# The second FFN's up projection from seven products of quarters, with weight sums made by adding transfers in DRAM

## The chip, the cores and the metric

The kernel runs on one core of one Trainium2 chip. The metric is the device time of one execution in microseconds; several runs are made, and their median counts. The engines are TensorE (PE, with its weight loads, PEld), VectorE (DVE), ScalarE (ACT), GpSimd (POOL), and SyncE (SP), which issues the loads.

## What is computed

A block of two layers over 512 latent tokens and 256 context tokens, 1024 channels wide, all in float32. Layer 0 mixes by gated convolutions, layer 1 by windowed attention; each is followed by an FFN with a short convolution:

```python
def conv_ffn(h, w_up, conv, w_down):
    u = dwconv(h @ w_up, conv)              # w_up: 1024 x 5632, three taps along the tokens
    a, g = jnp.split(u, 2, axis=-1)
    return (jax.nn.silu(g) * a) @ w_down    # w_down: 2816 x 1024

x = x + g1 * y                              # y: the mixer of the layer
x = x + g2 * conv_ffn(modulate(rmsnorm(x, norm_ffn[l]), sh2, sc2), w_up[l], w_conv_ffn[l], w_down[l])
```

The modulation (shift, scale, gate) is a matrix product of the conditioning with `w_mod`. The second layer's FFN sees the 512 latent tokens alone.

## The kernel before

Activations lie with channels on the partitions: eight tiles of 128 channels by the tokens. Every float32 operand of a large product is split into two `float32r` tiles: `split` lets ACT make the high part (L159) and DVE the low part (L160). `mm3` (L175) then makes one product of a 128 x 128 weight block by three matmuls: low weight by high input, high by low, high by high (L177 to L179).

A weight tile of 128 rows by 1024 is loaded by SP into one of three buffers `wraw` (L165, in `weights`) and split; the loads run one tile ahead of the products.

`run` goes through the stages: `start` (x, the first modulation pieces through `mod_piece`, the norm, the first projections), `layer0_input` and `layer0_output` (the convolution mixer: the taps on DVE at L578, pads of `ub` zeroed by POOL at L568, a sum `cs` made by POOL at L584 that `conv_norm` reads at L622), the first FFN (`ffn(0)`, 776 columns: 512 and 256), attention, and the second FFN (`ffn(1)`, 512 columns). POOL's small work in `inverse` (L296 to L301) stands in front of each norm.

In `ffn` the 22 pairs f of up-projection tiles (part 0 is `a`, part 1 is `g`) run in five groups (`GROUPS`: 4, 4, 4, 5 and 5 pairs). For the second FFN the first three pairs are made by `side_by_side` in halves of 256 columns, as the halves of h become ready; each other pair takes two `wide_gemm`s of 8 x 3 = 24 matmuls of 512 columns. `conv3` (L368 on ACT, L370 twice on DVE) is done for each part, then silu (L704), a product (L705) and a split give g. After the first pair of the next group, the eight output tiles of the group before are projected down (`down`: split, matmuls, `gate_in` at L360). The last group goes through `project`. `mod_rows` makes modulation columns that are wanted later out of rows of `w_mod` on DVE (L254, `wmod` loads at L250), a row at a time from a list `todo` that `do` works off.

The order of each engine's instructions is fixed when the kernel is built. A scheduler goes through the program by its own estimate of the times; an engine that is free takes the earliest instruction of the program that has its operands and its buffer. `tc.issue_after(ins)` adds an order to that: by its definition in the framework, what its block traces on the engine of `ins` is queued behind `ins`, and instructions of other engines in the block are left as they are. `self.mark` is the last split's instruction on DVE (L160).

## Time and profile before

| | us |
|---|---|
| median of 3 runs | 1472.71 (1472.37 to 1472.92) |
| the profiled execution, its own time | 1473.53 |
| its span, first to last instruction | 1471.8 |
| TensorE busy in the span | 1435.4 |
| DVE busy in the span | 1024.4 |
| mean granted TensorE clock | 0.997 of full |

The page shows one profiled execution. A busy PE is not a PE at its peak, since matmuls overlap: the distance from the start of one to the start of the next tells what one costs. What a stage is bound by is read from the stage's own stretch and not from the share of the whole span.

### The profile page before, as it was taken

How to read it: one execution, taken by the hardware profiler on the slowest of the kernel's cores; microseconds unless marked ns; L12 is line 12 of the kernel's file. 1: busy time of each engine (PE TensorE's matmuls, PEld its weight loads, DVE VectorE, ACT ScalarE, POOL GpSimd, SP SyncE). 2: the span in 40 equal slices, each digit the busy share in tenths (PEclk: the TensorE clock that was granted, in tenths of full speed). 3: DMA queues.
4: the chain of work that ended last, by engine and by line, in shares of the span. 5: the costliest groups of instructions: out<-in, count | busy, mean ns of one | idle time of the engine just before them, and what ended most of it. 6: DMA issues, size and time to landing. Idle time of an engine off the chain costs nothing.

```text
span 1471.8 us, 21937 instructions
## 1 busy us (share of the span) xinstructions
PE 1435.4 (98%) x8786; PEld 1228.8 (83%) x8786; DVE 1024.4 (70%) x1635; ACT 596.9 (41%) x983; POOL 47.8 (3%) x186
## 2 busy tenths in 40 slices
PE   5999999999999999999999999999999999999997
PEld 3888888888888888888888878768799888888887
DVE  6699998689977756456434689786676865655456
ACT  5421224463223223133123475786764442424245
POOL 0000001110000000000000110010001000000000
PEclk9999999999999999999999999999999999999999
DMA  9325433134544532333211324011155333233222
GB/s 374 111 70 173 158 115 130 31 113 146 168 132 127 186 106 81 120 125 91 81 47 43 106 91 125 14 40 58 42 174 163 90 112 98 84 114 97 94 80 74
DMA packets 52709, 161.25 MB, mean 110 GB/s; under 512 B 6400, under 2 KB 6528, under 8 KB 52480
## 3 DMA queue, kind: packets, MB, share of 16 engines
q1 hardware_dynamic: 52608, 159.87, 33.4%
q8 instruction: 68, 1.11, 0.3%
q14 instruction: 33, 0.27, 0.1%
HBM read 155.13 MB, written 2.10 MB: 107 GB/s over the span
## 4 chain that ended last, share of the span: by engine, by line
PE 91%; DVE 4%; ACT 2%; issue 1%; DMA 1%; POOL 1%; DVEq 0%; SPq 0%; ACTq 0%; POOLq 0%
PE slot L177 21%; PE slot L178 21%; PE slot L179 21%; PE av L178 3%; PE av L177 3%; PE av L179 3%; PE av L929 2%; PE pt L919 2%; PE s L900 2%; PE pt L179 2%; PE pt L178 2%; PE pt L177 2%; PE slot L226 1%; PE slot L212 1%; PE slot L208 1%
## 5 line engine op out<-in xcount | busy, mean ns | idle before, releaser
L177 PE MATMUL slot<-h,wlo 128*128 128x512 f32 (+1 forms) x1192 | 410.5, 346 | 2.2 <-DVE ub L570 1.2
L178 PE MATMUL slot<-h,whi 128*128 128x512 f32 (+1 forms) x1192 | 410.8, 345 | 0.2 <-DVE h L350 0.2
L179 PE MATMUL slot<-h,whi 128*128 128x512 f32 (+1 forms) x1192 | 410.8, 345 | 0.0
L159 ACT CAST whi<-wraw 128x1024 fp32r<-128x1024 f32 (+2 forms) x215 | 192.2, 902 | 208.5 <-PE slot L179 109.3
L177 PEld LDWEIGHTS slot<-h,wlo 128*128 128x128 f32 x1192 | 223.5, 188 | 34.3 <-issue 2.0
L178 PEld LDWEIGHTS slot<-h,whi 128*128 128x128 f32 x1192 | 224.1, 188 | 29.0 <-DVE h L350 0.5
L179 PEld LDWEIGHTS slot<-h,whi 128*128 128x128 f32 x1192 | 224.1, 188 | 27.6
L160 DVE TENSOR_TENSOR wlo<-wraw,whi 128x1024 fp32r<-128x1024 f32 (+2 forms) x215 | 222.2, 1040 | 25.1 <-ACT whi L159 24.6
L370 DVE SCALAR_TENSOR_TENSOR cf<-slot,par,cf 128x775 f32<-128x775 f32 (+1 forms) x132 | 122.7, 932 | 136.5 <-ACT cf L368 136.0
L177 PE MATMUL slot<-gh,wlo 128*128 128x512 f32 (+1 forms) x459 | 156.7, 342 | 0.7 <-DVE x L360 0.4
L178 PE MATMUL slot<-gl,whi 128*128 128x512 f32 (+1 forms) x459 | 155.5, 339 | 0.0
L179 PE MATMUL slot<-gh,whi 128*128 128x512 f32 (+1 forms) x459 | 155.1, 339 | 0.0
L368 ACT ACTIVATE cf<-slot,par 128x776 f32<-128x776 f32 (+1 forms) x66 | 55.3, 837 | 243.1 <-PE slot L179 230.7
L360 DVE SCALAR_TENSOR_TENSOR x<-slot,mod,x 128x256 f32<-128x256 f32 (+1 forms) x139 | 81.8, 618 | 73.6 <-PE slot L179 73.4
L578 DVE SCALAR_TENSOR_TENSOR cacc<-ub,par,cacc 128x783 f32<-128x783 f32 x120 | 118.6, 1040 | 0.2
L254 DVE CUSTOM_DVE_ANT_0 junk<-wmod,cb 128x1024 bf16<-128x1024 f32 x80 | 97.7, 1221 | 10.2 <-DMA wmod<-in_wmt 6.6
L177 PEld LDWEIGHTS slot<-gh,wlo 128*128 128x128 f32 x459 | 86.1, 188 | 12.0 <-DVE wlo L160 0.7
L178 PEld LDWEIGHTS slot<-gl,whi 128*128 128x128 f32 x459 | 86.4, 188 | 10.3 <-DVE mod L235 0.2
L179 PEld LDWEIGHTS slot<-gh,whi 128*128 128x128 f32 x459 | 86.4, 188 | 10.1
L907 DVE CUSTOM_DVE_ANT_0 sm<-s,mask,nsink 128x640 f32<-128x640 f32 (+1 forms) x58 | 46.8, 820 | 15.9 <-PE pt L919 12.4
L704 ACT ACTIVATE sgf<-cf 128x776 f32<-128x776 f32 (+1 forms) x44 | 32.7, 744 | 60.9 <-DVE cf L370 60.4
L910 ACT ACTIVATE sm<-sm,nm 128x513 f32<-128x513 f32 (+1 forms) x64 | 50.1, 786 | 10.6 <-DVE nm L907 5.6
(244 smaller groups left out, 2246.4 us busy)
## 6 DMA issues: line engine op xcount, KB each, us to landing
wraw<-in_w_up SPq DMA_DIRECT2D x88, 512.0 KB, 3.6
wmod<-in_wmt SPq DMA_DIRECT2D x56, 512.0 KB, 4.2
wmod<-in_wm SPq DMA_DIRECT2D x40, 512.0 KB, 5.3
wraw<-in_w_down SPq DMA_DIRECT2D x48, 256.0 KB, 2.6
wraw<-in_w_in SPq DMA_DIRECT2D x20, 512.0 KB, 4.0
wraw<-in_w_down SPq DMA_DIRECT2D x32, 320.0 KB, 2.9
wraw<-in_w_o SPq DMA_DIRECT2D x16, 512.0 KB, 3.4
wraw<-in_w_out SPq DMA_DIRECT2D x16, 256.0 KB, 3.4
```

Of the source, the lines that this page charges most:

```text
L159: self.act_mark = self.nc.scalar.copy(hi, src)
L160: self.mark = self.nc.vector.tensor_tensor(lo, src, hi.bitcast(F32), op=ALU.subtract)
L177: mm(out, lo, xh, start=first, stop=False)
L178: mm(out, hi, xl, start=False, stop=False)
L179: self.product = mm(out, hi, xh, start=False, stop=last)
L254: nc.vector.tensor_tensor_reduce(junk, w, self.cb[:, c, :], 1.0, 0.0, ALU.mult, ALU.add, col)
L360: self.nc.vector.scalar_tensor_tensor(self.x[k][:, lo:hi], acc, self.mod[:, l, chunk * 8 + k, c:c + 1], self.x[k][:, lo:hi], op0=ALU.mult, ...
L368: nc.scalar.activation(acc[:, :n], u[:, :n], AF.Copy, scale=w[:, 1:2])
L370: nc.vector.scalar_tensor_tensor(acc[:, o], u[:, i], w[:, j:j + 1], acc[:, o], op0=ALU.mult, op1=ALU.add)
L578: self.tapped = nc.vector.scalar_tensor_tensor(acc, ub[:, t:t + CB_N], w[:, t:t + 1], acc, op0=ALU.mult, op1=ALU.add)
L907: scored = nc.vector.tensor_tensor_reduce(sm[:, :n], s[:, SEQ - nl:SEQ + CTX], mk, -SCALE, nsink[:, hd:hd + 1], ALU.add, ALU.min, nm)
L910: self.scored = scored, nc.scalar.activation(sm[:, :n + 1], sm[:, :n + 1], AF.Exp, scale=-1.0, bias=nm, accum_out=z)
```

## The change

For the pairs f = 3 to 21 of the second FFN, the two tiles of a pair and the 1024 input channels (even and odd tiles) form a 2 x 2 block matrix, and so do the input channels and the two halves of the 512 tokens. Strassen's scheme (in Winograd's form) makes the product from seven products of quarters instead of eight: `seven` makes each by 4 x 3 matmuls of 256 columns, and adds the parts partly in PSUM (two products into one bank) and partly by ACT and DVE into `ua` and `ug` in SBUF, which `conv3` then reads.

The sums of the input quarters are made by `quarters` at the start of the second FFN on DVE (th, tl; the unsplit h is kept by `raw`). The sums of the weight quarters (s1 to s4) are made in DRAM by transfers that POOL issues (`weight_sums`): for each of 19 pairs four plain copies and four adding ones, 128 x 512 values each, in six steps of which each waits for the one before. `ffn(0)` takes a step of the generator after each of its 41 later up projections, inside `issue_after(self.mark.ins)`. `load_seven` loads seven quarters of a pair (six transfers) into four `wraw` tiles instead of two tiles, and `next_seven` splits them, a pair ahead.

With it go: the layer-1 rows 40 to 47 of `mod_rows` move from the second FFN's start into the first FFN's list; the down projections of a group are spread over the pairs of the next (`DOWNS`) between products; the last group's weights m = 4 to 7 use the buffers of the input sums; eight g tiles are kept instead of six; the host orders the columns of `w_up[1]` by even and odd tiles.

```diff
+FEW = 3
+DOWNS = {
+    **{4 * grp + 4 + i: [(grp, 2 * i), (grp, 2 * i + 1)] for grp in range(3) for i in range(4)},
+    17: [(3, 0), (3, 1), (3, 2)], 18: [(3, 3), (3, 4), (3, 5)], 19: [(3, 6), (3, 7)],
+}
...
-                    self.ffn(1, HALVES, 6)
+                    self.ffn(1, HALVES, 8)
...
+        self.dram = self.pool("dram", space=bass.MemoryType.DRAM)
...
+        t = self.tmp.tile([P, T], F32, name="ht", tag="tC") if raw is None else raw(k, lo)
...
+    def weight_sums(self):
+        dma = self.nc.gpsimd.dma_start
+        w = self.a["w_up"][1]
+        add = dict(accum_op=ALU.add)
+        self.sums = {}
+        def pair(f):
+            a11, a21, a12, a22 = (w[f, i, :, j:j + 512] for i, j in ((0, 0), (0, 512), (1, 0), (1, 512)))
+            s1, s3 = (self.dram.tile([P, 512], F32, name=t, tag=f"{t}_{f}") for t in ("s1", "s3"))
+            s24 = self.dram.tile([P, 1024], F32, name="s24", tag=f"s24_{f}")
+            s2, s4 = s24[:, 0:512], s24[:, 512:1024]
+            self.sums[f] = s1, s24, s3
+            dma(s1, a21)
+            dma(s3, a11)
+            yield
+            dma(s1, a22, **add)
+            dma(s3, a21, **add)
+            yield
+            dma(s2, s1)
+            yield
+            dma(s2, a11, **add)
+            yield
+            dma(s4, s2)
+            yield
+            dma(s4, a12, **add)
+        under = []
+        todo = deque(range(FEW, NF))
+        while todo or under:
+            if todo:
+                under.append(pair(todo.popleft()))
+            under = [b for b in under if next(b, self) is None]
+            yield
+    def load_seven(self, f):
+        w = self.a["w_up"][1][f]
+        s1, s24, s3 = self.sums[f]
+        for parts in ((w[0][:, :512], s1), (s24,), (s3, w[1][:, :512]), (w[1][:, 512:],)):
+            raw, n = self.wts.tile([P, 1024], F32, name="wraw", tag="wraw", bufs=3), 0
+            for p in parts:
+                self.nc.sync.dma_start(raw[:, n:n + p.shape[1]], p)
+                n += p.shape[1]
+            yield raw[:, :n]
...
+    def next_seven(self, raws, out, first=False):
...
+                n = raw.shape[1]
+                self.split(raw, hi[:, :n], lo[:, :n])
+                out.extend((hi[:, j:j + 512], lo[:, j:j + 512]) for j in range(0, n, 512))
+            yield
...
+    def seven(self, f, parts, h, then, early, late):
+        nc = self.nc
+        xa, va, ya = (self.slot()[:, :256] for _ in range(3))
+        ua, ug = (self.ph.tile([P, SEQ], F32, name=n, tag=f"{n}{f % 2}") for n in ("ua", "ug"))
+        q = lambda t, i: t[:, 256 * i:256 * i + 256]
+        b = {n: [(q(x[0], i), q(x[1], i)) for x in src] for n, src, i in (
+            ("11", h[0::2], 0), ("21", h[1::2], 0), ("22", h[1::2], 1),
+            *((n, list(zip(self.th, self.tl)), i) for i, n in enumerate(("n1", "t3", "n2", "t4"))))}
+        lo, hi = slice(0, 256), slice(256, 512)
+        def product(acc, w, n, start=False):
+            for k in range(4):
+                self.mm3(acc, w, k, *b[n][k], start and k == 0, k == 3, not start)
+        a11, s1, s2, s4, s3, a12, a22 = parts
+        product(xa, a11, "11", True)
+        nc.scalar.copy(ua[:, lo], xa)
+        product(va, s1, "n1", True)
+        nc.scalar.activation(ug[:, hi], va, AF.Copy, scale=-1.0)
+        then()
+        early()
+        product(xa, s2, "n2")
+        nc.scalar.copy(ua[:, hi], xa)
+        product(va, s4, "22")
+        nc.vector.tensor_tensor(ua[:, hi], ua[:, hi], va, op=ALU.add)
+        then()
+        product(ya, a12, "21", True)
+        nc.vector.tensor_tensor(ua[:, lo], ua[:, lo], ya, op=ALU.add)
+        product(xa, s3, "t3")
+        nc.vector.tensor_tensor(ug[:, hi], ug[:, hi], xa, op=ALU.subtract)
+        then()
+        late()
+        product(xa, a22, "t4")
+        nc.scalar.activation(ug[:, lo], xa, AF.Copy, scale=-1.0)
+        then()
+        return ua, ug
...
     def ffn(self, l, segs, ng):
...
-        conds = 2 - l
-        self.cb = self.ph.tile([P, conds, DM], F32, name="cb")
-        nc.sync.dma_start(self.cb, a["cc_row"][0:conds].partition_broadcast(P))
-
-        def silu():
-            with self.tc.issue_after(self.act_mark.ins):
-                nc.scalar.activation(self.cb, self.cb, AF.Silu)
-
-        self.todo.append(silu)
-        self.mod_rows(l, 40, 4, conds)
-        self.mod_rows(l, 44, 4, conds)
         if l == 0:
+            self.cb = self.ph.tile([P, 2, DM], F32, name="cb")
+            nc.sync.dma_start(self.cb, a["cc_row"].partition_broadcast(P))
+
+            def silu():
+                with self.tc.issue_after(self.act_mark.ins):
+                    nc.scalar.activation(self.cb, self.cb, AF.Silu)
+
+            self.todo.append(silu)
+            self.mod_rows(0, 40, 4, 2)
+            self.mod_rows(0, 44, 4, 2)
             self.mod_rows(1, 0, 16, 2)
             self.todo.append(lambda: self.make_gain(2, 1, 1, self.p("nmix")[:, 8:16], 0, 8))
             self.mod_rows(1, 16, 24, 1)
             self.todo.append(lambda: self.make_gain(3, 1, 4, self.p("nffn")[:, 8:16], 0, 8, 1))
+            self.mod_rows(1, 40, 8, 1)
         ups = [(f, part) for f in range(NF) for part in range(2)]
-
-        self.do(11 if l else 3)
+        if l:
+            self.quarters()
+
+        self.do(3)
         done = [self.slot() for _ in self.pre]
         self.side_by_side(done, h, segs)
         nf = len(done)
-        with self.tc.issue_after(self.marks[0].ins), self.tc.issue_after(self.marks[1].ins):
-            ahead = self.weights(a["w_up"][l, ups[nf][0], ups[nf][1]], into=self.spare(0))
+        if l == 0:
+            sums = self.weight_sums()
             with self.tc.issue_after(self.marks[0].ins), self.tc.issue_after(self.marks[1].ins):
...
+        else:
+            ahead = []
+            for _ in self.next_seven(self.load_seven(FEW), ahead, True):
+                pass
...
+            if l and f >= FEW:
+                now, ahead = ahead, []
+                then = self.next_seven(self.load_seven(f + 1), ahead) if f + 1 < NF else iter(())
+                head = deque(partial(down, *t) for t in DOWNS.get(f, ()))
+                fresh = any(f == grp[0] for grp in GROUPS)
+                early = lambda: [head.popleft()() for _ in range(0 if fresh else len(head) // 2)]
+                late = lambda: head and head.popleft()()
+                u = self.seven(f, now, h, lambda: next(then, None), early, late)
+                for t in head:
+                    t()
...
                     self.wide_gemm(s, w, h, whole)
                     self.do(1)
+                    with self.tc.issue_after(self.mark.ins):
+                        next(sums, None)
...
-                if grp < 2:
-                    self.do(1)
+            if grp < 3:
+                self.do(1)
...
+            room = {4: partial(self.spare, 0), 5: partial(self.spare, 1), 7: cb, 6: partial(self.spare, i, TW, ("gh", "gl"))}
+        else:
+            room = {4 + p: partial(self.quarter_room, p) for p in range(4)}
...
+    def quarters(self):
+        nc = self.nc
+        self.th, self.tl = [], []
+        for p, raw in enumerate(self.raw):
+            b = raw.rearrange("p (q n) -> p q n", q=4)
+            t, u = (self.tmp.tile([P, T], F32, name="qs", tag=g)[:, :SEQ] for g in ("tA", "tB"))
+            nc.vector.tensor_tensor(
+                t.rearrange("p (q n) -> p q n", q=2), b[:, 0:3:2, :], b[:, 1:2, :].broadcast_to([P, 2, 256]), op=ALU.subtract)
+            nc.vector.scalar_tensor_tensor(u[:, :256], t[:, :256], -1.0, b[:, 2, :], op0=ALU.mult, op1=ALU.subtract)
+            nc.vector.scalar_tensor_tensor(u[:, 256:], u[:, :256], -1.0, b[:, 3, :], op0=ALU.mult, op1=ALU.subtract)
+            hi, lo = self.quarter_room(p)
+            for i, src in enumerate((t, u)):
+                self.split(src, hi[:, 512 * i:512 * i + 512], lo[:, 512 * i:512 * i + 512])
+            self.th.append(hi)
+            self.tl.append(lo)
...
+    even_odd = d["w_up"][1, FEW:].reshape(NF - FEW, 2, P, KT // 2, 2, P).transpose(0, 4, 2, 1, 3, 5)
+    d["w_up"][1, FEW:] = even_odd.reshape(NF - FEW, 2, P, DM)
```

## Rows read from the trace of the kernel before

**Rows 1.** The page's head and its section 4, the chain of work that ended last.
```profile
PE 1435.4 (98%) x8786; PEld 1228.8 (83%) x8786; DVE 1024.4 (70%) x1635; ACT 596.9 (41%) x983; POOL 47.8 (3%) x186
...
PE 91%; DVE 4%; ACT 2%; issue 1%; DMA 1%; POOL 1%; DVEq 0%; SPq 0%; ACTq 0%; POOLq 0%
```

**Rows 2.** Timeline of PE, second FFN: start us, us, instruction; products 512, then 256 columns wide.
```profile
1143.17 0.39 PE L178 MATMUL slot<-h,whi 128*128 128x512 f32 x1
...
1148.61 0.39 PE L178 MATMUL slot<-h,whi 128*128 128x512 f32 x1
...
1089.78 0.28 PE L178 MATMUL pt<-ol,whi 128*128 128x256 f32 x1
...
1094.58 0.28 PE L179 MATMUL slot<-oh,whi 128*128 128x256 f32 x1
```

**Rows 3.** Stretches of 20 us, second FFN: busy us (instructions) by engine, clock, DMA share, GB/s.
```profile
1120.00:1140.00 20.00, 19.75 (x129) 17.79 (x127) 13.42 (x20) 6.95 (x9) 0.00 (x0) 1.00 0.59 185
1140.00:1160.00 20.00, 19.75 (x86) 15.62 (x85) 20.00 (x33) 12.35 (x20) 0.00 (x0) 1.00 0.34 92
...
1240.00:1260.00 20.00, 20.00 (x90) 16.57 (x89) 10.30 (x13) 6.15 (x8) 0.00 (x0) 1.00 0.21 75
```

**Rows 4.** Groups of 1143 to 1430 us by shape: count, busy us, mean ns of one.
```profile
L160 DVE TENSOR_TENSOR wlo<-wraw,whi 128x1024 fp32r<-128x1024 f32 x34 | 41.4, 1219 | 6.5 <-ACT whi L159 6.5
L370 DVE SCALAR_TENSOR_TENSOR cf<-slot,par,cf 128x511 f32<-128x511 f32 x40 | 29.9, 751 | 27.1 <-ACT cf L368 26.7
L160 DVE TENSOR_TENSOR wlo<-wraw,whi 128x512 fp32r<-128x512 f32 x24 | 16.5, 686 | 0.0
```

**Rows 5.** Timeline of DVE, ACT and PE around the start of the second FFN.
```profile
1080.57 0.48 DVE L360 SCALAR_TENSOR_TENSOR x<-slot,mod,x 128x256 f32<-128x256 f32 x1
1119.35 0.42 DVE L160 TENSOR_TENSOR h<-ht,h 128x256 fp32r<-128x256 f32 x1 [0.78 <-ACT h L159]
1121.72 1.23 DVE L254 CUSTOM_DVE_ANT_0 junk<-wmod,cb 128x1024 bf16<-128x1024 f32 x1 [1.95 <-ACT cb L666]
...
1130.35 0.40 PE L178 MATMUL slot<-h,whi 128*128 128x512 f32 x1
```

**Rows 6.** Stretches of 10 and 20 us from the kernel's start; columns as in rows 3.
```profile
0.00:10.00 10.00, 0.00 (x0) 0.00 (x0) 3.19 (x11) 5.45 (x6) 0.20 (x4) 1.00 0.81 280
10.00:20.00 10.00, 5.51 (x68) 4.64 (x72) 6.16 (x18) 4.81 (x8) 0.00 (x0) 1.00 1.03 410
20.00:30.00 10.00, 6.50 (x93) 3.54 (x84) 9.90 (x16) 6.47 (x11) 0.00 (x0) 1.00 1.03 408
30.00:40.00 10.00, 10.00 (x111) 8.39 (x110) 5.94 (x10) 5.73 (x11) 0.00 (x0) 1.00 1.01 401
...
140.00:160.00 20.00, 20.00 (x167) 17.05 (x166) 18.55 (x21) 4.24 (x6) 0.00 (x0) 1.00 0.48 174
```

**Rows 7.** Timeline of the start: SP's queue, then PE's first matmuls and its last modulation piece.
```profile
0.74 4.12 SPq L121 DMA_DIRECT2D x<-in_x  x8
...
13.30 14.27 SPq L222 DMA_DIRECT2D wmod<-in_wm  x12
...
14.49 2.72 PE L291 MATMUL slot<-ones,ss 128*128 128x2 f32 x12 [14.49 <-DVE ss L284]
...
41.17 1.93 PE L226 MATMUL slot<-wmod,csil 128*2 128x128 f32 x64
```

**Rows 8.** Tile `ones` (its one memset, its reader), then POOL's timeline (rows of memset and sum).
```profile
L615 DVE MEMSET ones<- x1: 165/165/165, 52.4 to 52.4; 128x128 f32 x1
L622 PE MATMUL slot<-cs,ones x4: 380/538/592, 218.4 to 250.7; 128*128 128x512 f32 x2, 128*128 128x256 f32 x2
...
42.76 0.56 POOL L568 MEMSET ub<- 128x15 f32 x12 [42.32 <-PE slot L226]
191.01 1.89 POOL L584 TENSOR_TENSOR cs<-cacc 128x783 f32<-128x783 f32 x1 [147.69 <-DVE cacc L578]
237.03 0.20 POOL L296 TENSOR_SCALAR ry<-rv 128x4 int32<-128x4 int32 x1 [44.14 <-ACT rv L294]
```

**Rows 9.** The page's sections 3 and 6: DMA queues; loads, KB each, us from issue to landing.
```profile
q1 hardware_dynamic: 52608, 159.87, 33.4%
...
wmod<-in_wm SPq DMA_DIRECT2D x40, 512.0 KB, 5.3
wraw<-in_w_down SPq DMA_DIRECT2D x48, 256.0 KB, 2.6
```

**Rows 10.** Stretches of 20 us in the first FFN; columns as in rows 3.
```profile
500.00:520.00 20.00, 20.00 (x118) 17.70 (x118) 8.85 (x15) 1.24 (x2) 0.00 (x0) 1.00 0.53 171
680.00:700.00 20.00, 20.00 (x120) 17.78 (x119) 11.36 (x15) 6.91 (x9) 0.00 (x0) 1.00 0.18 50
```

More of the change, by code (lines that the diff above doesn't have):

```diff
@@ L172, in spare, with mm3 @@
         return [self.ph.tile([P, n], F32R, name=t, tag=f"{t}{i}") for t in tags]
-    def mm3(self, out, w, k, xh, xl, first, last):
+    def mm3(self, out, w, k, xh, xl, first, last, more=False):
         hi, lo = (t[:, k * P:(k + 1) * P] for t in w)
-        mm = self.nc.tensor.matmul
+        mm = partial(self.nc.tensor.matmul, skip_group_check=more)
         mm(out, lo, xh, start=first, stop=False)
@@ new lines, in load_seven @@
+    def load_seven(self, f):
[8 more added lines that the diff above has]
+    def next_seven(self, raws, out, first=False):
+        for i, raw in enumerate(raws):
+            if i == 0 and first:
+                for j in range(2):
+                    hi, lo = (self.ph.tile([P, SEQ], F32R, name=t, tag=f"{t}{4 + j}") for t in ("gh", "gl"))
+                    self.split(raw[:, 512 * j:512 * j + 512], hi, lo)
+                    out.append((hi, lo))
+            else:
+                if i == 3:
+                    hi, lo = (self.act.tile([P, DM], F32R, name=f"{t}2") for t in ("whi", "wlo"))
+                else:
+                    hi, lo = (self.wts.tile([P, 1024], F32R, name=t, tag=t, bufs=3) for t in ("whi", "wlo"))
+                n = raw.shape[1]
+                self.split(raw, hi[:, :n], lo[:, :n])
+                out.extend((hi[:, j:j + 512], lo[:, j:j + 512]) for j in range(0, n, 512))
+            yield
@@ L681, in ffn @@
         nf = len(done)
-        with self.tc.issue_after(self.marks[0].ins), self.tc.issue_after(self.marks[1].ins):
-            ahead = self.weights(a["w_up"][l, ups[nf][0], ups[nf][1]], into=self.spare(0))
+        if l == 0:
+            sums = self.weight_sums()
+            with self.tc.issue_after(self.marks[0].ins), self.tc.issue_after(self.marks[1].ins):
+                ahead = self.weights(a["w_up"][l, ups[nf][0], ups[nf][1]], into=self.spare(0))
+        else:
+            ahead = []
+            for _ in self.next_seven(self.load_seven(FEW), ahead, True):
+                pass
         g = []
@@ L692, in up @@
                     s = done[i]
+                elif l:
+                    s = u[part]
                 else:
@@ L706, in up, with down @@
             g.append(self.pair(f % ng, sg, n, n))
-        def down(grp):
-            for m in range(KT):
-                w = self.weights(a["w_down"][l][grp][m], len(GROUPS[grp]) * P, self.spare(m % 3) if m % 3 < 2 else None)
-                s = self.slot()
-                self.wide_gemm(s, w, g[GROUPS[grp][0]:GROUPS[grp][-1] + 1], whole)
-                for lo, hi in whole:
-                    self.gate_in(m, s[:, lo:hi], l, 5, lo, hi)
-                if grp < 2:
-                    self.do(1)
+        def down(grp, m):
+            room = (self.spare(m % 3) if m % 3 < 2 else None) if l == 0 else self.late_room(m % 2)
+            w = self.weights(a["w_down"][l][grp][m], len(GROUPS[grp]) * P, room)
+            s = self.slot()
+            self.wide_gemm(s, w, [g[f] for f in GROUPS[grp]], whole)
+            for lo, hi in whole:
+                self.gate_in(m, s[:, lo:hi], l, 5, lo, hi)
+            if grp < 3:
+                self.do(1)
         for grp, fs in enumerate(GROUPS):
@@ L720, in ffn @@
                 up(f)
-                if grp and f == fs[0]:
-                    down(grp - 1)
+                if l == 0 and grp and f == fs[0]:
+                    for m in range(KT):
+                        down(grp - 1, m)
         self.do(len(self.todo))
@@ L937, in output, with raw @@
         room = [[self.act.tile([P, DM], F32R, name=f"{t}{i}") for t in ("whi", "wlo")] for i in range(3)]
-        half = self.project(a["w_o"], DM, o, HALVES[1:], 1, 2, few=(1, 3))
-        self.tokens_in_turn(HALVES, half, (3, 1, 3), [w[f, part] for f in range(3) for part in range(2)], 0, room)
+        self.raw = [self.shifted(self.act, "th", p, F32) for p in range(KT // 2)]
+        def raw(k, lo):
+            t = self.raw[k // 2]
+            if k % 2 == 0:
+                return t[:, 0:512]
+            return t[:, 768:1024] if lo == 0 else t[:, 256:768]
+        half = self.project(a["w_o"], DM, o, HALVES[1:], 1, 2, few=(1, 3))
+        self.tokens_in_turn(
+            HALVES, half, (3, 1, 3), [w[f, part] for f in range(3) for part in range(2)], 0, room, raw)
+    def quarters(self):
[13 more added lines that the diff above has]
+            self.tl.append(lo)
     def turned(self, seg):
```

24 lines of the change are left out of this document (15 added, 9 removed).

## The prediction

> **What bounds the kernel now.** First the page: TensorE is busy for 98% of the span, and 91% of the chain that ended last is PE [rows 1]. Next PE's own timeline, since a busy PE says nothing of what one matmul costs. From the first to the last quoted start at 512 columns lie 24 matmuls in 5.44 us, 0.2267 us each; at 256 columns 40 in 4.80 us, 0.120 us each [rows 2]. Half the columns cost 53% of the time, not 50%. Then the stretches: in the second FFN PE is full while DVE has 10.3 of 20 us to do (1240 to 1260), but at the stage's entry (1140 to 1160) DVE is full too [rows 3]. Last the start of the kernel, which the change doesn't seem to touch: there the 16 DMA engines are at a share of 1.01 to 1.03 from 10 to 40 us, and PE is idle for the first 10 us [rows 6].
>
> **Products (the gain).** A pair f = 3 to 21 now takes 48 matmuls of 512 columns: 48 x 0.2267 = 10.88 us. The seven products take 7 x 4 x 3 = 84 of 256: 84 x 0.120 = 10.08 us. That is 0.80 us a pair, 19 x 0.80 = **-15.2 us**, 7.4% of these products where the count of operations alone would give 12.5%. The Trainium skill ("TensorE: Matmul & The Clock Gate", Back-to-back issue gap) gives N / 2.4 + 2.5 ns for a warm matmul: by it the pair would go from 10.36 to 9.17 us, the gain would be an estimated 22.6 us, and the final sum 1474. The spacings above show some 13 ns on top of N / 2.4, not 2.5, so the rows decide.
>
> **More DVE and ACT work in the second FFN.** Per pair, DVE splits 3.5 tiles of 1024 instead of 2: +1.22 +0.69 us [rows 4], and adds three PSUM parts of 256 columns, nearest row 0.48 us each [rows 5]: +3.3 us. Its whole list for a pair without down projections is then 3 x 1.22 + 0.69 (splits) + 3 x 0.48 + 4 x 0.75 (conv) + 2 x 0.69 (product and split of g) = 10.2 us by durations, against 10.08 us of PE. With two down projections PE has 2 x 12 x 0.2267 = 5.4 us more and DVE 2 x (0.69 + 0.75) = 2.9. So over the stage it fits: 19 x 10.2 = 194 us, 32 down projections of 1.44 us 46, against 19 x 10.08 + 92 = 284 of PE (92: 24 down projections of 12 and 8 of 15 matmuls, at 0.2267). The entry is where it is tight. DVE finishes h at 1119.8 and PE starts f = 3 at 1130.35 [rows 5]. `mod_rows` is gone from there (8 x 1.23 = 9.8 us, moved to the first FFN, where PE is full and DVE has 8.9 to 11.4 us of 20 [rows 10]: nothing for it), and `quarters` comes in: four times 0.69 + 2 x 0.48 + 2 x 0.69 = 3.0, together 12.1 us. Until the first down projection (two pairs later, 1150.5) DVE must do 12.1 + two pairs' splits 8.7 + the conv chains of f = 0 to 3 at 4.4 each, 17.5, + 1.4 = 39.7 us in 30.7. It is late by up to 9 us; the next pair's products can be put in between at 1.2 us of split for 2.9 us of PE. I take +3, between 0 and +9. Where two products share a bank, an addition stands between them (0.48 us and two hand-overs); the down projection covers it except in f = 3, 16, 20 and 21: +1, between 0 and +4. Together **+4 us** (0 to +13). Nothing else is seen: SP issues six loads a pair (1.75 MB) instead of two at a DMA share of 0.21 to 0.34 in this stage [rows 3]; the last group's late weights wait for the input sums' buffers to the end of f = 21, but four of its output tiles come before them (10.8 us of products).
>
> **Where the weight sums run.** This decides the sign. `weight_sums` issues 19 x 8 = 152 transfers of 256 KB (39.8 MB) on POOL. The tie is `issue_after(self.mark.ins)`, and `self.mark` is on DVE: by its definition the block orders only what it traces on DVE, and there it traces POOL's transfers alone. So I read the tie as empty. Their sources are inputs and their targets DRAM tiles of their own, so the 38 first copies are ready at time zero. An engine that is free takes what is ready, however far ahead: the memset of `ones` (L615) ran at 52.4 us for a first reader at 218, and POOL zeroed the pads of all four `ub` at 42.8 [rows 8]. POOL has nothing to do before. I expect the sums from about 1 us on, in the stretch where the DMA engines have no room [rows 6], and not in the first FFN, where the share is 0.18 to 0.53 [rows 10].
>
> **Price at the start.** SP moves x (3.1 MB), parameters, 16 modulation transfers and three weight tiles before the last modulation piece is complete, 13.5 MB: by the stretches of rows 6 (2.8 + 4.1 + 4.1 by 30 us) that is at 36 us, and PE uses it at 41.2 [rows 7], so 5 us are spare. All loads use one queue now [rows 9]; no row shows what a second one takes. Below: nothing, if it gets only what the first leaves. Above: half. With half of 0.41 MB/us the 13.5 MB take 66 us: 30 later, less 5, +25. If SP keeps two thirds (its rows are 4 KB, those of the sums 2 KB): 49 us, +8. I take the middle of these two, **+17 us**, since the adding transfers read twice and a shared queue seems nearer than a yielding one. The Trainium skill ("DMA: Bandwidth & Descriptors", Issuing engines are not separate DMA queues) says that transfers issued from any engine run on the same 16 engines and interleave. By that rule the zero end falls away and the sum stands at 1481.5 rather than 1464.5; no run here shows it yet.
>
> **After the start.** At 0.41 MB/us the sums need 97 us of all engines, 146 if an adding transfer costs double. SP's share is about 0.48 (140 to 160, [rows 6]), so from some 58 us on about half is free: done at 190 to 283 us. A landing of 5.3 us (`wmod`, [rows 9]) may become 8 to 10, mostly behind a tile loaded ahead (24 such loads pass through two buffers). And POOL waits in order: an adding transfer waits for its copy, and behind it are the pads at 42.8, the sum `cs` at 191 that PE reads at 218, and `inverse` at 237 [rows 8]. I take **+3 us** (0 to +25, below).
>
> **Sum.** 1473.5 (own time of the profiled run) - 15.2 + 4 + 17 + 3 = 1482.3; that run is 0.8 over the median of the runs shown, so **1481.5 us**, +0.6%. Alone this case reaches from 1470 to 1493.
>
> **Rivals.**
> 1. The sums cost nothing: SP's queue goes first, or the transfers do run in the first FFN as the title has it (there 8 x 0.26 MB in a step of 8.3 us are a share of 0.62 beside 0.18 to 0.53). For it: PE has tiles ahead everywhere after 60 us. Against: the empty tie and rows 6. Time: 1473.5 - 15.2 + 4 - 0.8 = **1461.5**. This is the other side: faster. It decides from a start that stretches by less than 8 us.
> 2. Adding transfers cost double, and POOL falls behind: with PE at 218 + 17 = 235 us only 29 + 177 x 0.52 = 121 of 146 us are done, and `cs` waits for the remaining 25. Time: 1481.5 - 3 + 25 = **1503.5**. For it: two reads and a write. Against: the scheduler may have put `cs` ahead.
> 3. DVE becomes the bound of the second FFN: 9 us at the entry and 0.3 us in each of 19 pairs, 15 instead of 4; with the sums free, **1472.5**. Against: 0.6 of DVE's time in the stage as it stands.
>
> **How the numbers follow.** Forecast 0.42, rival 1 0.30, rival 2 0.20, rival 3 0.08. A change of 0.2% (2.9 us) is about what can be told from none. Faster: 0.27 of rival 1, 0.01 of rival 3: 0.28. Same: 0.10 of the forecast's lower end, 0.03 of rival 1, 0.04 of rival 3: 0.17. Slower: the rest, 0.55. The range must take in both signs: 1459 leaves out a tenth below (the lower part of rival 1), 1507 about a tenth above.
>
> **What would show it.** The tie: a second DMA queue with 152 transfers whose first rows stand near 1 us (right) or past 309 us (wrong). The start: PE's first matmul later than 14.5 us [rows 7], the last modulation piece's matmuls (64 of L226) at about 58 instead of 41.2. POOL: `cs` and the first `inverse` late by more than the start is, and PE waiting for them, is rival 2. The products: 84 matmuls at 0.120 us a pair, and 284 us from f = 3 to the last group instead of 299. DVE: PE idle before `seven`'s products between 1130 and 1165. The prediction is wrong if the transfers stand in the first FFN, or if the start is as long as before.

## The result, and the profile after

The changed kernel takes 1541.15 us (median of 4, 1539.47 to 1543.16) against 1472.82: **slower by 4.6%**, ratio 1.0464 with a 95% interval of 1.0446 to 1.0482. The prediction said 1481.5 (1459 to 1507): the right sign, and 60 us too little.

The page of the changed kernel, its first line, its two large DMA queues, and the shares of the chain that ended last:

```profile
PE 1436.9 (93%) x9470; PEld 1255.4 (82%) x9470; DVE 1085.6 (71%) x1750; ACT 651.8 (42%) x1105; POOL 148.6 (10%) x338
...
q1 hardware_dynamic: 63408, 174.29, 34.7%
q0 software_dynamic: 17024, 39.86, 11.5%
...
PE 73%; DVE 10%; issue 7%; POOL 4%; DMA 3%; ACT 3%; DVEq 0%; SPq 0%; ACTq 0%; POOLq 0%
```

PE held 91% of the chain before [rows 1] and holds 73% now. DVE, POOL and "issue" (waits without a named cause, here those in front of POOL's transfers) have most of the rest. The new queue q0 carries the 152 transfers: 11.5% of 1539.3 us is 177 us of all 16 engines.

POOL's timeline of the changed kernel (start us, us, line, operation, and the idle time before it), to be held against [rows 8]:

```profile
1.26 0.74 POOL L675 DMA_DIRECT2D s<-in_w_up  x1 [0.82 <-POOLq L1230]
...
4.58 0.55 POOL L675 DMA_DIRECT2D s<-in_w_up  x1
7.89 0.54 POOL L676 DMA_DIRECT2D s<-in_w_up  x1 [2.76 <-issue]
...
121.10 1.00 POOL L576 MEMSET ub<- 128x15 f32 x12
...
259.01 0.81 POOL L687 DMA_DIRECT2D s<-in_w_up  x1 [0.72 <-issue]
259.64 2.13 POOL L592 TENSOR_TENSOR cs<-cacc 128x783 f32<-128x783 f32 x1
...
308.02 0.61 POOL L304 TENSOR_SCALAR ry<-rv 128x4 int32<-128x4 int32 x1 [46.24 <-ACT rv L302]
```

The first transfer stands at 1.26 us, the last at 259: the tie holds nothing back. The pads of `ub` come at 121.1 where they came at 42.8, `cs` at 259.6 in place of 191.0, and the first `inverse` 71 us late. What that did to the other engines stands in the stretches (10 and 20 us: busy time of PE, PEld, DVE, ACT, POOL, granted clock, DMA share, GB/s):

```profile
10.00:20.00 10.00, 0.00 (x0) 0.00 (x0) 4.18 (x5) 3.60 (x5) 3.67 (x7) 1.00 1.03 398
100.00:120.00 20.00, 6.75 (x42) 5.88 (x40) 0.00 (x0) 0.00 (x0) 9.18 (x13) 0.78 0.93 156
120.00:140.00 20.00, 9.88 (x42) 8.29 (x43) 17.04 (x19) 3.72 (x4) 9.55 (x25) 0.62 0.88 161
```

And in the waits of ACT and DVE (who for whom: us in total, times, longest):

```profile
ACT cacc L583 <- POOL ub L576: 31.0, 1, 31.0
DVE cacc L586 <- ACT cacc L583: 30.6, 1, 30.6
```

PE does nothing yet from 10 to 20 us, where before it was at work [rows 6]; its first matmul comes at 21.7 instead of 14.5 us. From 100 to 120 us DVE does nothing at all: its taps wait for ACT, ACT for the pads. From 100 to 140 us PE is busy for only 6.8 and 9.9 of 20 us, and its granted clock averages 0.78 and 0.62 there, between its levels of 2.4 and 1.2 GHz. The taps, 120 of about 1.03 us that bound this stage, begin at 122.8 instead of 61.7.

The lateness against the kernel before, read at POOL's `inverse` in front of each norm and at the end:

| | before | after | late by |
|---|---|---|---|
| first norm (mixer) | 237.0 | 308.0 | 71.0 |
| last norm ahead of the first FFN | 300.3 | 375.7 | 75.3 |
| norm ahead of attention | 837.5 | 912.9 | 75.4 |
| last norm ahead of the second FFN | 1103.9 | 1180.7 | 76.8 |
| end | 1471.8 | 1539.3 | 67.5 |

So 71.0 of the 76.8 us are lost before 308 us and 4.3 more up to 376 (the runs do not say by what); the first FFN and attention hand the loss on, and the second FFN, which the change is about, gets 9.3 us shorter.

### The profile page after: what moved, and what is told of

Its sections match the earlier page's. It is cut to its first block, busy times and chain, and to the rows that moved or that the text cites. A ratio compares the mean times of both kernels' runs of the same rounds, so it can differ in the third digit from the quotient of the medians.

```text
span 1539.3 us, 23963 instructions
## 1 busy us (share of the span) xinstructions
PE 1436.9 (93%) x9470; PEld 1255.4 (82%) x9470; DVE 1085.6 (71%) x1750; ACT 651.8 (42%) x1105; POOL 148.6 (10%) x338
## 3 DMA queue, kind: packets, MB, share of 16 engines
q0 software_dynamic: 17024, 39.86, 11.5%
## 4 chain that ended last, share of the span: by engine, by line
PE 73%; DVE 10%; issue 7%; POOL 4%; DMA 3%; ACT 3%; DVEq 0%; SPq 0%; ACTq 0%; POOLq 0%
PE slot L185 17%; PE slot L186 17%; PE slot L187 17%; DVE cacc L586 4%; PE av L1079 2%; PE pt L1069 2%; DVE wlo L167 2%; PE s L1050 2%; PE av L185 2%; PE av L186 2%; PE av L187 2%; DMA wraw<-in_w_down 1%; PE pt L185 1%; PE pt L187 1%; PE pt L186 1%
## 5 line engine op out<-in xcount | busy, mean ns | idle before, releaser
L185 PE MATMUL slot<-h,wlo 128*128 128x256 f32 (+1 forms) x1152 | 388.2, 339 | 38.2 <-DVE ub L578 24.5
L186 PE MATMUL slot<-h,whi 128*128 128x256 f32 (+1 forms) x1152 | 386.4, 336 | 0.0
L187 PE MATMUL slot<-h,whi 128*128 128x256 f32 (+1 forms) x1152 | 385.8, 335 | 0.0
L166 ACT CAST whi<-wraw 128x1024 fp32r<-128x1024 f32 (+2 forms) x249 | 219.7, 892 | 237.0 <-PE slot L187 88.7
L167 DVE TENSOR_TENSOR wlo<-wraw,whi 128x1024 fp32r<-128x1024 f32 (+2 forms) x249 | 254.9, 1028 | 89.7 <-ACT whi L166 88.7
L186 PEld LDWEIGHTS slot<-h,whi 128*128 128x128 f32 x1152 | 219.5, 191 | 23.8 <-DVE xr L344 0.7
L187 PEld LDWEIGHTS slot<-h,whi 128*128 128x128 f32 x1152 | 219.2, 190 | 22.9 <-issue 0.7
L378 DVE SCALAR_TENSOR_TENSOR cf<-slot,par,cf 128x775 f32<-128x775 f32 (+1 forms) x92 | 92.6, 1009 | 108.1 <-ACT cf L376 108.0
L185 PE MATMUL slot<-gh,wlo 128*128 128x512 f32 (+1 forms) x435 | 148.4, 343 | 2.0 <-ACT gh L166 1.1
L186 PE MATMUL slot<-gl,whi 128*128 128x512 f32 (+1 forms) x435 | 147.9, 341 | 0.0
L187 PE MATMUL slot<-gh,whi 128*128 128x512 f32 (+1 forms) x435 | 147.6, 340 | 0.0
L376 ACT ACTIVATE cf<-slot,par 128x776 f32<-128x776 f32 (+1 forms) x46 | 41.4, 900 | 201.9 <-PE slot L187 197.8
```

The lines of the kernel that those rows point to most:

```text
L166: self.act_mark = self.nc.scalar.copy(hi, src)
L167: self.mark = self.nc.vector.tensor_tensor(lo, src, hi.bitcast(F32), op=ALU.subtract)
L185: mm(out, lo, xh, start=first, stop=False)
L186: mm(out, hi, xl, start=False, stop=False)
L187: self.product = mm(out, hi, xh, start=False, stop=last)
L376: nc.scalar.activation(acc[:, :n], u[:, :n], AF.Copy, scale=w[:, 1:2])
```

## The experiments

Two theories stood: **POOL's order** (small work of POOL queued behind transfers) and **shared DMA engines** (late loads). Against both: the transfers are not the cause, and the second FFN or its scheduling is.

**Transfers left out, and transfers alone.** e1_no_sums is the changed kernel with these lines:

```diff
-            sums = self.weight_sums()
+            sums = iter(())
...
-        s1, s24, s3 = self.sums[f]
+        s1, s24, s3 = w[1][:, :512], w[0], w[0][:, 512:]
```

> The changed kernel without its 152 transfers: the second FFN loads quarters of the weights themselves where the sums would be, in the same six loads a pair. It leaves the weight sums out, so its output is not the reference's. If the whole loss comes from the transfers (by way of POOL's order or of the DMA engines), the start is the one of before (first matmul at 14.5 us, pads at about 43, cs at about 191) and only the second FFN's gain is left: in the changed kernel the stages' distance to before falls from 77.0 us at the second FFN's entry to 67.5 at the end, 9.5 us, so 1472.8 - 9.5 = about 1463 us. If the products or their entry cost more than that, the time lies between 1466 and 1475. If the loss has nothing to do with the transfers, about 1541.

e2_sums_only is the kernel before with `weight_sums` and, in the first FFN's `up`:

```diff
                     self.do(1)
+                    with self.tc.issue_after(self.mark.ins):
+                        next(sums, None)
```

> The kernel before with the 152 transfers added to it under the same tie and nothing else: nobody reads the sums, the second FFN is the old one. If the transfers alone carry the loss: 1541 + 9.5 = about 1550 us, pads near 121 and cs near 260 us. If the loss needs the new second FFN (or its scheduling), the time stays near 1473 to 1485.

Measured: 1464.46 us without the transfers (ratio 0.9937, 0.9922 to 0.9952, beside a before of 1473.71), 1550.54 with the transfers alone (1.0527, 1.0511 to 1.0542). The transfers cost 1541.15 - 1464.46 = 76.7 us in the new kernel and 1550.54 - 1473.71 = 76.8 in the old one. So the transfers account for all of the loss, and the rest of the change gains 9.3.

**POOL's work moved out of the queue.** e3_pads_on_dve changes one word, e6_pads_cs_dve another one as well:

```diff
-            nc.gpsimd.memset(ub[:, lo:lo + n], 0.0)
+            nc.vector.memset(ub[:, lo:lo + n], 0.0)
...
-            self.taps[1].append(lambda: nc.gpsimd.tensor_tensor(self.cs, self.cacc[0], acc, op=ALU.add))
+            self.taps[1].append(lambda: nc.vector.tensor_tensor(self.cs, self.cacc[0], acc, op=ALU.add))
```

> The changed kernel with the zeroing of the four ub tiles' pads on DVE in place of POOL (12 memsets of 15 columns, 0.4 us each before); transfers, their order and cs stay as they are. Theory POOL's order: in the changed kernel the pads stand at 121 us because some 70 transfers are queued ahead of them, the DVE chain of 120 taps starts at 122.8 instead of 61.7, and that is the larger half of the loss. Then the taps start with the data, about 31 us later than in the kernel before (the lateness of the last modulation piece), at about 93, and the time falls by about 30 to about 1511. Theory DMA engines alone: the values that the taps need come late anyway, the pads are not what is waited for, and the time stays at 1541 within 5 us.

> The changed kernel with both things that stand on POOL in the start on DVE: the pads of ub and the sum cs (783 columns, 1 to 2 us of DVE). The transfers keep their empty tie and run from 1 us. With the pads alone moved (1519.4 us) the taps ended at 247.7, 26.6 us later than before, while cs came only at 272.6, right behind POOL's last transfer. If POOL's order makes that second wait: cs follows the taps, the lateness at the first inverse falls from 53 to about 27 us, and the time to about 1492 (1488 to 1500); what is then left over 1464.5, some 28 us, is the price of the DMA engines shared with the loads of the start. If the loads themselves are what is late there: 1515 to 1520.

Measured: 1519.39 us with the pads moved, 1518.42 with both. The pads behind the transfers cost 21.8 us, less than the 30 expected; `cs`, though it came at 272.6 in e3, costs 1.0, which the scatter of e3's runs (1513.8 to 1522.4) doesn't tell from nothing. The 1492 expected for e6 did not come: with nothing of the mixer but its `inverse` on POOL, 54.0 us over e1 remain, and the last two taps begin only 25.4 us late (245.8 against 220.5). Another 25 are lost between there and the first `inverse` (287.0 against 236.5), which here waits for its input and not for POOL. The tile `wmod` between 60 and 300 us says where; first e1, then e6 (loads: first and last start; landing, the time from issue to arrival; who waited):

```profile
L230 SPq DMA_DIRECT2D wmod<-in_wm x22: 327/341/1830, 109.5 to 205.3; - x22
...
DMA to landing us min/median/max: 3.4/4.3/5.7
```

```profile
L230 SPq DMA_DIRECT2D wmod<-in_wm x24: 327/328/422, 76.3 to 260.1; - x24
...
  PE slot L234: 9.9, 6
...
DMA to landing us min/median/max: 5.0/7.3/10.8
```

These loads pass through two buffers, so one can't start before PE has used the one before the last. Landing in 7.3 us instead of 4.3, they become a chain of their own, its last load starts at 260 instead of 205, and PE, full in e1 from 100 to 240 us, waits for them.

**From where on the engines are shared.** e10_after_start is e6 with the transfers tied to the first accumulator, which exists from 58 us on:

```diff
         self.glu(0, sl[0], sl[1])
+        tie = nc.gpsimd.tensor_copy(self.tmp.tile([P, 6], F32, name="tie", tag="rt")[:, 0:1], self.cacc[0][:, 0:1])
+        with self.tc.issue_after(tie.ins):
+            for _ in self.weight_sums():
+                pass
```

> The changed kernel with pads and cs on DVE (1518.4 us with transfers from 1 us on), and the transfers tied to a POOL copy of the first conv accumulator, which exists from about 58 us: the start keeps the DMA engines to itself, the modulation loads between 60 and 290 us share them. It splits the 54 us between that run and the kernel without transfers (1464.5) into its two halves. By that run's stages (28 us late where the taps end, 50 late at the first inverse): the start's part is about 29 and the later part about 25, so here about 1464.5 + 25 = 1490 us, with the taps no later than in the kernel before and the first inverse late by about 25 us. If all of the lateness comes from the start and the later stage only hands it on: 1465 to 1470. If the later stage pays for as many bytes as the start did: 1500 to 1518.

Measured: 1540.21 us, in place of 1490. The start is as before (taps from 61.3 to 220.8 us), and yet the first `inverse` is 72 us late. POOL's timeline:

```profile
306.37 1.67 POOL L691 DMA_DIRECT2D s<-in_w_up  x2 [1.19 <-DMA s<-s]
308.18 0.19 POOL L304 TENSOR_SCALAR ry<-rv 128x4 int32<-128x4 int32 x1
```

PE's longest wait up to 450 us:

```profile
PE slot L331 <- DVE rd L321: 48.6, 2, 47.8
```

And a stretch of 20 us:

```profile
280.00:300.00 20.00, 0.00 (x0) 0.00 (x0) 0.00 (x0) 0.00 (x0) 9.82 (x15) 0.50 0.93 173
```

This time the `inverse` itself stood behind the transfers, and PE was empty for their sake. e12_after_start_no_pool takes it off POOL:

```diff
-            nc.scalar.copy(rs[i], self.rstd(ss, [(0, n)], self.ones2b, at))
+            nc.scalar.copy(rs[i], self.rstd(ss, [(0, n)], self.ones2b, at, eng=nc.vector))
```

> The kernel of the last run but one (transfers from 61 us on, pads and cs on DVE, 1540.2 us) with the first two inverses (the conv norm's, 13 operations of 2 and 4 columns each) on DVE in place of POOL, so that nothing of the start or the mixing stage stands on POOL behind the transfers. There POOL's last transfer came at 306.4 and the first inverse right behind it at 308.2; DVE waited 44.7 us for it and PE 47.8, with PE empty from 280 to 300 us. Theory POOL's order: the first inverse follows its own input at about 263, and the time falls by 45 to 48 us to about 1494, which leaves some 27 to 30 us over the 1464.5 without transfers as the price of the shared DMA engines in the mixing stage. If the stage were held by its loads as well, the time falls by less than 20 us, to 1520 or more.

Measured: 1493.83 us, as expected of POOL's order; the first `inverse` stands on DVE at 260.05. So the engines shared from 61 us on cost 1493.83 - 1464.46 = 29.4 us. Up to 3 us of that is still order: the third `inverse`, left on POOL, has its input at 310.8 and begins behind the last transfer at 314.0. The start's part follows by subtraction, 1518.42 - 1493.83 = 24.6; it was not run alone, and the transfers end some 44 us later in e12 than in e6, so the split is rough.

The loads of `wmod` are not all of the 29.4. In e12 SP waits 29.0 us for landings before it can load `wmod` again (8.0 in e1), but PE waits for `wmod` itself only 6.5 us. The output projection's weights land in 6.4 us instead of 3.1, and DVE waits for their splits, 22.7 us in place of 1.1 (60 to 320 us):

```profile
DVE wo L167 <- ACT wo L166: 22.7, 7, 8.2
```


**What an adding transfer costs.** e7_plain_copies:

```diff
-        add = dict(accum_op=ALU.add)
+        add = {}
```

> The changed kernel with the 95 adding transfers as plain copies (so the weight sums are not sums, and the output is not the reference's): the same 152 transfers, bytes and order. The page puts 177 us of all engines on the 39.86 MB of that queue, where the loads of the other queue would take 97 us for as many bytes. If adding is the dear part: that queue's time falls to about 100 us, the last transfer from 259 to about 190, the pads from 121 to about 90, and the time by 30 to 50 us to some 1495 to 1510. If a transfer from DRAM to DRAM costs that much with or without the addition: within 10 us of 1541.

Measured: 1505.10 us. Queue q0 of its page:

```profile
q0 software_dynamic: 12160, 39.86, 7.6%
```

That is 7.6% of 1506.9 us, 114.5 us for 152 copies, 0.753 each. Half of the transfers are additions, four of each pair's eight, so 76 (the expectation's 95 is a miscount). With them it was 177.0 us: (177.0 - 76 x 0.753) / 76 = 1.58 us for an addition, 2.09 times a copy. Packets point the same way: 12160 / 152 = 80 for a copy, and (17024 - 76 x 80) / 76 = 144 for an addition, 1.8 times. The last transfer is issued at 175.7, the pads stand at 90.4, and the time falls by 36.

**Room for descriptors.** e8_ring2048:

```diff
-dynamic_dma_scratch_size=1024
+dynamic_dma_scratch_size=2048
```

> The changed kernel with twice the descriptor room for POOL's transfers (2048 in place of 1024 bytes a partition; all tiles move by 1024 bytes). In the changed kernel POOL issues seven transfers back to back and from then on waits 0.5 to 4 us before each, for nothing that the profile shows. If it waits for room: about 14 go out at once, POOL runs some 7 transfers (about 11 us) further ahead, the pads come at about 110 and the time falls by about 10 to 1531. If it waits for the earlier transfer that it reads from, or the start gets still less of the engines: 1541 to 1550.

Measured: 1524.22 us, 17 less, where 10 were expected. POOL's timeline there:

```profile
5.10 0.54 POOL L676 DMA_DIRECT2D s<-in_w_up  x1
7.26 0.53 POOL L675 DMA_DIRECT2D s<-in_w_up  x1 [1.62 <-DMA s<-in_w_up]
...
106.69 0.89 POOL L576 MEMSET ub<- 128x15 f32 x12
...
218.33 0.81 POOL L687 DMA_DIRECT2D s<-in_w_up  x1 [1.62 <-issue]
```

Eight go out at once instead of seven, not 14. POOL's waits without a name in front of transfers fall from 153.7 us (eight lines of its waits in the changed kernel, together) to 25.9, and 87.0 us of waits for an earlier transfer's landing come in, also in front of copies that read inputs alone. So most of the nameless waits were for room; with more of it another limit on the transfers under way comes next. POOL ends 41 us earlier all the same, and the pads come 14 earlier.

**A tie that binds.** e4_real_tie:

```diff
+            self.tie = self.cst.tile([P, 1], F32, name="tie")
...
-                    with self.tc.issue_after(self.mark.ins):
+                    tie = nc.gpsimd.tensor_copy(self.tie, w[1].bitcast(F32)[:, 0:1])
+                    with self.tc.issue_after(tie.ins):
                         next(sums, None)
```

> The changed kernel with a tie that binds: at each step of the first FFN POOL first copies one column of that step's split weight tile (a copy that has to wait for DVE's split), and the block that orders the transfers is tied to this copy, which is on POOL itself, the engine that issues them. The transfers then run from about 310 us on, in a stretch where POOL has nothing else to do and the DMA share was 0.18 to 0.53. If place and order of the transfers are the whole loss: start and stages up to 305 us as before, the first FFN unchanged, the second FFN 9.5 us shorter, about 1463 us, faster than before. If an adding transfer costs its time wherever it runs (DMA engines taken from the weight loads): the first FFN grows by 10 to 60 us, 1475 to 1525 us.

Measured: 1478.94 us, 62 less than the changed kernel, but 14.5 over e1. The transfers run from 312 us on, and PE is full in the first FFN, also where the DMA share is over 1:

```profile
340.00:380.00 40.00, 40.00 (x228) 34.81 (x227) 37.90 (x53) 15.36 (x19) 19.87 (x28) 1.00 1.05 298
```

Its matmuls are slower. Groups by shape of e4 (count, busy us, mean ns of one), 700 to 760 us, h against `wlo` and gl against `whi`:

```profile
L185 PE MATMUL slot<-h,wlo 128*128 128x512 f32 x18 | 7.1, 396 | 0.0
...
L186 PE MATMUL slot<-gl,whi 128*128 128x512 f32 x40 | 15.6, 389 | 0.0
```

In e1 they take 391 and 389. In e4 the new tile moved the weight tiles by 32 bytes (gh and gl with them) while h stayed. e11_before_shifted puts that one tile into the kernel before, and e5_tie_in_place takes it out of e4:

```diff
+        nc.vector.memset(self.cst.tile([P, 1], F32, name="more"), 0.0)
         self.mod = self.cst.tile([P, 2, 48, 2], F32, name="mod")
```

> The kernel before with one 32-byte tile more among its constants and nothing else (one memset of one column on DVE): all weight tiles of the first FFN and of the mixing stage move by 32 bytes, h stays, so that their addresses differ by 32 modulo 64 bytes, as in the run with the first binding tie. Theory placement: 512-column matmuls of h against whi take 395 ns in place of 390 and start 0.234 us apart in place of 0.228, the 256-column ones 282 in place of 279; with some 1056 of each in the first FFN that is 5.8 + 2.6 us there, 3 to 4 in the mixing stage, and about 1483 to 1486 us in all. If the slower matmuls of that run came from the transfers (none here): 1473.

```diff
-                    tie = nc.gpsimd.tensor_copy(self.tie, w[1].bitcast(F32)[:, 0:1])
+                    tie = nc.gpsimd.tensor_copy(self.tmp.tile([P, 6], F32, name="tie", tag="rt")[:, 0:1], w[1].bitcast(F32)[:, 0:1])
```

> The binding tie once more, with the copied column put into a tile that the kernel already has (rt) in place of a new 32-byte tile of its own. In the run with the new tile (1478.9 us) PE was full in the first FFN and yet every 512-column matmul of h against whi took 395 ns in place of 390, every 256-column one 282 in place of 279, while those of gl against whi kept 392 and 389; the new tile had moved all weight tiles by 32 bytes against h. Theory placement: with the weights where they were, h against whi is back at 390 and 279, and the time is the 1464.5 us of the kernel without transfers, at most 4 above it (1464 to 1469). Theory contention: the 152 transfers in the first FFN cost the 9 to 15 us by themselves, and the time stays at about 1479.

Measured: e11 1487.44 us, 13.8 over its before of 1473.68 (ratio 1.0094, 1.0081 to 1.0108), without one transfer and a little over the 1483 to 1486 expected: 5.0 us are lost before the first FFN and 8.6 in it. e4 loses 4.5 and 9.0 against e1 in the same stretches, so the 32 bytes explain nearly all of its 14.5 us, and the transfers cost hardly anything there.

e5 takes 1471.49 us (11 runs, 1466.64 to 1475.45; ratio 0.9987, 0.9976 to 0.9998), above the 1464 to 1469 of the placement theory and below the 1479 of the other. Its matmuls are back at 390 and 279, but it stays 7.0 over e1, its first FFN 8.5 (545.7 against 537.2). DVE's waits in that first FFN, and the same two in e4:

```profile
DVE junk L262 <- DMA wmod<-in_wmt: 27.5, 12, 6.7
...
DVE wlo L167 <- POOL tie L845: 11.0, 2, 7.0
```

```profile
DVE junk L262 <- DMA wmod<-in_wmt: 28.1, 12, 7.0
...
DVE wlo L167 <- POOL tie L846: 2.2, 1, 2.2
```

A stretch of 40 us in e5:

```profile
500.00:540.00 40.00, 38.13 (x214) 33.29 (x213) 24.35 (x38) 8.52 (x10) 15.59 (x25) 0.96 1.02 303
```

DVE stands in order behind modulation rows that land late, and two splits wait for POOL's copy to have read the weight tile. The first wait is as long in e4, where PE is full; the second is the one that e5 has more of. That points to the copy, but e4's slower matmuls also leave the other engines more time, and the two were not run apart. e9_paced is meant to take both away: every third output tile, of the down projections too, releases one step, and the copy reads a column that DVE clears in its own order:

```diff
+        def pay():
+            steps[0] += 1
+            if steps[0] % 3 == 0:
+                at, tie = (self.tmp.tile([P, 6], F32, name=t, tag=t)[:, 0:1] for t in ("rv", "rt"))
+                with self.tc.issue_after(self.mark.ins):
+                    nc.vector.memset(at, 0.0)
+                tie = nc.gpsimd.tensor_copy(tie, at)
+                with self.tc.issue_after(tie.ins):
+                    next(sums, None)
```

> A binding tie that is paced and that holds no weight tile: in the first FFN every third output tile, of the up and the down projections, releases one step of the sums; DVE clears one column after its split (tied to that split, which is on DVE), POOL copies the column, and the transfers are tied to POOL's copy. In the run before, with a step at every up projection (1471.5 us), the DMA share stood at 1.00 to 1.05 from 340 to 580 us, the rows of the modulation landed in 6.6 us instead of 4.4 (DVE waited 27.5 us for them in all), two splits waited 11.0 us for POOL's copy of a weight column, and the first FFN took 545.7 us in place of 537.2. If these waits are what stood between 1471.5 and the 1464.5 of the kernel without transfers: the 152 transfers spread over some 500 us, the share stays at 0.6 to 0.9, the first FFN is back at 537 to 539, and the time is 1465 to 1467, faster than before by 0.5%. If the sums cost their time in the first FFN however they are spread: 1469 to 1473.

Measured: **1465.23 us** (5 runs, 1463.89 to 1465.52), ratio to before 0.9940 (0.9928 to 0.9953): 0.6% faster than the kernel before, and 0.8 over the kernel without transfers, which the runs do not tell from none. Its first and last transfer on POOL's timeline:

```profile
332.84 0.74 POOL L675 DMA_DIRECT2D s<-in_w_up  x1
...
779.16 0.81 POOL L687 DMA_DIRECT2D s<-in_w_up  x1 [0.16 <-issue]
```

Three stretches of 40 us:

```profile
460.00:500.00 40.00, 40.00 (x234) 35.29 (x233) 29.21 (x46) 12.03 (x16) 13.09 (x20) 1.00 0.85 238
500.00:540.00 40.00, 40.00 (x230) 35.18 (x229) 24.68 (x38) 8.27 (x9) 11.75 (x19) 1.00 0.95 284
...
580.00:620.00 40.00, 40.00 (x234) 35.26 (x233) 24.63 (x41) 7.68 (x10) 14.19 (x23) 1.00 1.04 306
```

PE is full at shares of 0.85 to 1.04, though DVE still waits 25.2 us in all for modulation rows: no single wait there is longer than 3.6 us, where in e5 one was 6.7. No split waits for POOL's copy any more. The pace and the new tie were changed together; what each brings was not run.

## Why the prediction was wrong, step by step

Over e1's 1464.46 us the loss comes apart into four differences between runs. They belong to the order in which things were taken out; another order could divide the sum otherwise.

| what | by | us | predicted |
|---|---|---|---|
| engines shared in the start | e6 - e12 | 24.6 | 17 (0 to 25) |
| engines shared behind it | e12 - e1 | 29.4 | part of 3 (0 to 25) |
| `cs` behind the transfers | e3 - e6 | 1.0 | part of the same 3 |
| pads behind the transfers | after - e3 | 21.8 | part of the same 3 |

**Products and the second FFN: right, 2 us too good.** -15.2 + 4 = -11.2 was forecast; e1 gives -9.3, the changed kernel's own stage -9.3. PE loses 4.0 us at the entry (16.93 of 20 us busy from 1130 to 1150 in e9, 19.03 from 1150 to 1170; 0.5 in the kernel before), inside the 0 to 13 of that term. Over the whole stage PE's listed waits are 7.9 us in e9 and 0.9 before, 7.0 more where +4 was taken: enough for the missing 2, though no run changes that term alone.

**The empty tie: right.** It decided the sign, as said: an order tied to an instruction of DVE holds nothing that POOL issues.

**The start: right in kind, a middle taken where the upper end held.** 24.6 us of the 0 to 25. Packets, MB and share by queue in the changed kernel, from 5 to 30 us and then from 0 to 60:

```profile
q0 software_dynamic: 1502, 4.72, 51.9%
q1 hardware_dynamic: 1758, 4.99, 51.2%
```

```profile
q1 hardware_dynamic: 3811, 12.20, 52.9%
q0 software_dynamic: 3260, 9.33, 48.0%
```

From 5 to 30 us each queue got half of the bytes. Over 60 us SP's loads moved 0.20 MB/us, half of the 0.41 they had alone: the prediction's upper end, and not its middle between half and two thirds. The last modulation matmuls of the start stand at 72.3 us instead of 41.2, 31 later, where the prediction looked for 58. The Trainium skill ("DMA: Bandwidth & Descriptors", SWDGE vs HWDGE vs iDMA) says that an engine goes round its internal queues in turn and that the two kinds of issuers feed different ones; the bytes from 5 to 30 us agree.

**After the start: the step that failed**, +3 where 52.2 were lost, twice its own upper end. Three readings in it were wrong.
- "mostly behind a tile loaded ahead": the prediction saw that 24 loads of 512 KB pass through two buffers and that a landing might become 8 to 10 us (7.3 in e6), and still took the buffers for cover. Two buffers give one load of lead. Where neither DVE's taps nor PE have slack [rows 6], a landing longer by 3.0 us, two dozen times in a chain, is not covered; with the output projection's weights landing late behind it, the sharing costs 29.4 us. How much of that each of the two brings was not run.
- The pads. The row at 42.8 us was named among the things behind the transfers, and then given no price. They are 0.6 us of POOL's time, but DVE's taps, 120 x 1.03 us, can't begin without them, and 72 transfers stood in front. That cost 21.8 us.
- The drain. "Done at 190 to 283 us" was right (259). But it was used only to ask whether `cs` at 235 comes too late, not what else waits in that queue before.

**Rival 2 (1503.5, 0.20): the premise right, the place wrong.** An addition costs 2.09 copies (e7), and POOL does fall behind, but `cs` costs 1.0 us; the pads stand 148 us earlier in the same order [rows 8]. The Trainium skill ("Collectives: The Full Stack", The bandwidth ceiling: the fold count and why AG ≠ RS ≠ AR) explains a measured ratio of 1.93 between a copying and a reducing collective by the second source that is read; the 2.09 here and the packets, 144 to 80, fit that, but no run shows the cause.

**Rival 1 (1461.5, 0.30)** is what a binding, paced tie gives: 1465.2. **Rival 3** (DVE as the bound of the second FFN) did not come: its stage gained 9.3.

**The range** ended at 1507 because the forecast's upper ends and rival 2 were taken as alternatives. They happened together: sharing in the start, sharing behind it and the queue's order added up, while the DMA share stood at 0.88 to 1.06 in every stretch of 20 us up to 260.

## What to carry to other kernels

A tie must name an instruction on the engine that issues what it is to hold back; look in the trace for the first transfer's start before pricing anything else. When transfers move onto an engine's queue, list every other instruction on that queue, with who can't begin without it, and price each by that engine's wait and not by its own length. Background transfers belong where the DMA share is low: in the first FFN they cost 0.8 us when they were paced and held no weight tile, and 7.0 with neither (e5); which of the two matters is open. And before a slower run is put down to what was added, look whether the addition moved other tiles: e4's loss was nearly all placement.

## What the runs showed of the hardware

- Thirty-two bytes. Where the weight tiles stand 32 bytes further on against the moving tile h than in the kernel before, matmuls of 512 columns take 395 to 396 ns against 390 and of 256 columns 282 against 279, by the trace's groups; in the kernel before that is 13.8 us for one tile of one column (e11). Tiles that moved together (gh, gl and weights in e4) kept their 389 to 394. Only these two placements were run.
- An adding transfer from DRAM to DRAM takes 1.58 us of all 16 engines for 256 KB, a plain one 0.753, by the difference of two runs and both in company of other loads.
- A share of 1.0 of the DMA engines is not in itself a loss: in e9 PE stayed full from 580 to 620 us at a share of 1.04, and in e4 from 340 to 380 at 1.05.
